# Hybrid SSD, window-attention and expert block on one core: 64-row products padded to 128 rows, and products of 64 output rows issued in turn into both halves of the array

## The chip, the cores and the metric

The kernel runs on one core of one Trainium2 chip. The metric is the device time of one execution in microseconds (us), the median of several runs. The engines are TensorE (PE; its weight loads are listed apart, as PEld), VectorE (DVE), ScalarE (ACT), GpSimd (POOL), and SyncE (SP), whose queue issues most DMAs.

## The reference, cut to what matters

One layer over 512 tokens of width 1024: an SSD branch and a window-attention branch read the same projections, their outputs are merged, and a two-of-64 mixture of experts follows. The change touches these lines of SSD (4 groups G, 8 heads J in each, head width P = 64, state N = 128, chunks of L = 128 tokens) and of attention (16 heads of width 64, 4 key/value heads, blocks of 128 tokens):

```python
    # ssd_branch
    seg = a_cum[:, :, :, None] - a_cum[:, :, None, :]
    decay = jnp.exp(jnp.where(causal, seg, -jnp.inf)).astype(xs.dtype)
    cb = jnp.einsum('bclgn,bcsgn->bclsg', cm, bm)
    y_diag = jnp.einsum('bclsgj,bcsgjp->bclgjp', cb[..., None] * decay, xdt)
    ...
    # swa_sink_branch
    scores = jnp.einsum('bnqhgd,bnkhd->bnhgqk', qb, kk).astype(jnp.float32) * ATT_SCALE
    scores = jnp.where(mask[None, :, None, None], scores, -jnp.inf)
    ...
    p = (p / denom[..., None]).astype(v.dtype)
    out = jnp.einsum('bnhgqk,bnkhd->bnqhgd', p, vv)
    ...
    # hybrid_layer
    merged = jax.nn.sigmoid(g_ssd) * y_ssd + jax.nn.sigmoid(g_att) * y_att
    x = x + merged @ w_out
    y_moe = hier_moe(h2, ...)       # 64 experts, every token goes to two
```

## The kernel before

**Stages.** The program first normalises and transposes the input (L154 to L176) and then runs the front part: projections with weights that stream in by tiles of 1 MB (`proj`, L186 to L200, and `qkv_tile`, L470 to L486), SSD by groups (`ssd_main`, L322 to L404), attention by key/value heads (`att_stage`, L557 to L632), the merge (L680 to L695) and the output projection with the router's logits (L724 to L774). Then come routing and the expert part, which streams all 64 experts' weights, 192 tiles of 1 MB, through a ring of 4 tiles `ra` and 10 tiles `rb` (L777 to L790). The `ra` and `rb` tiles lie where the front part's tiles lay, so their first loads wait until those are read for the last time.

**Products.** A projection splits operands into a high and a low part in the type fp32r and sums three products (L197 to L199, 512 columns each; L483 to L485, 256 columns each). Products in plain fp32 stand in the trace as two records for one matmul.

**Products that use part of the array.** Four places use fewer than 128 rows or fewer than 128 output rows:

- `decay` (L365), once for each of the 32 SSD heads, spreads one row of the cumulated decay over 128 partitions. The row is held as a high part in partitions 0 to 31 and a low part in 32 to 63 of `aT`, and `sel` picks and adds the two, so the product contracts over 64 rows. Its output `sb` goes through DVE (L369) and ACT (L368, L374) to a matrix `M`.
- `head` (L391): for head u (0 or 1) of pair i, four products, one for each chunk, write 64 output rows into the lower (u = 0) or upper half (u = 1) of one tile `y`. The matrix `M` is multiplied by `cbm` first, on DVE for u = 0 and on GpSimd for u = 1 (L388). One decay is made ahead (`SSD_AHEAD` = 1).
- `scores` in attention (L573, L574): a query tile holds the high part of its 64 values in one half of the partitions and the low part in the other, and L573 multiplies 128 rows of it with a doubled key tile `kT`. L574 adds the high part of the query times the low part of the key, `kL`, over 64 rows. `kL` holds the low parts of two key/value heads, one in each half.
- `weigh` (L620): for each block n, four heads (pr, u), each with the own block's weights `pc` and, for n > 0, the previous block's `pp`, write 64 output rows into half u of the tile `po[pr]`.

**Order.** The stages are written one after the other (L644 to L677), and a scheduler that works at build time mixes them: between the products of SSD and attention it puts projection products of other stages on TensorE. What order results is fixed in the program. Each engine works its own list in order.

Of the kernel before, what the change touches and what calls it, by code (L numbers as in the profile page):

```python
# [21 lines left out]
CAP, BLK, NE, NBK, STEP = 32, 128, 64, 32, 512  # L22
POOL_LO, SSD_AHEAD, NA, NB, XGT, UX = 5, 1, 4, 10, 2, 8
PAD = 800

# [6 lines left out]
def tile_hybrid(ctx: ExitStack, tc: tile.TileContext, x, pos, cols, rows, g2d, wrd, wdtd, wcm, wqkv, wso, wao, wo,  # L32
# [7 lines left out]
    def ptile(tag, bufs=2, dt=F):  # L40
        return psum.tile([128, 512], dt, name=tag, tag=tag, bufs=bufs)
# [3 lines left out]
                                      for n in ("py", "pg", "pw", "px", "pb", "pc", "pz", "pv")]  # L45
    pz.tile([128, PAD], F, name="pad")


    jp = pb.tile([128, 128], F, name="jp")
    G.iota(jp, pattern=[[1, 128]], base=0, channel_multiplier=-1, allow_small_or_imprecise_dtypes=True)  # L50
# [3 lines left out]
    V.tensor_scalar(tri, jp, 0.0, None, op0=OP.is_ge)  # L54
    trs = pb.tile([128, 128], F, name="trs")
    V.tensor_scalar(trs, jp, 0.0, None, op0=OP.is_lt)
    mcur = pb.tile([128, 128], U8, name="mcur")
    V.tensor_scalar(mcur, jp, 0.0, None, op0=OP.is_le)
    one = cp.tile([128, 1], F, name="one")
    V.memset(one, 1.0)  # L60
# [6 lines left out]
    V.memset(half, 0.5)  # L67
    sel = pb.tile([64, 32], R, name="sel")
    V.tensor_tensor(sel, ident[0:64, 0:32], ident[0:64, 32:64], op=OP.add)
    colt = pb.tile([128, 168], F, name="colt")  # L70
# [16 lines left out]
    G.iota(io4, pattern=[[STEP, 8], [1, 32]], base=0, channel_multiplier=0, allow_small_or_imprecise_dtypes=True)  # L87
    io1 = cp.tile([128, 128], F, name="io1")
    G.iota(io1, pattern=[[1, 128]], base=0, channel_multiplier=0, allow_small_or_imprecise_dtypes=True)
# [11 lines left out]
    oneb = onec.to_broadcast([128, 128])  # L101
    ltb = cp.tile([128, 128], BF, name="ltb")
    V.tensor_scalar(ltb, jp, 0.0, None, op0=OP.is_gt)
    iot = io1[:, 0:64]
    rst = cp.tile([128, 2, 17], F, name="rst")
    gts = cp.tile([128, 48], F, name="gts")
    gw = cp.tile([128, 2, 4], F, name="gw")
    ohs = cp.tile([128, 2, 256], BF, name="ohs")
# [27 lines left out]
    def y_(dt=R): return tk(py, "y", 16, 512, dt)  # L136
    def b_(dt=F): return tk(px, "b", 8, 512, dt)
    def a_(dt=F): return tk(pa, "a", 8, 512, dt)
# [68 lines left out]
    nacum = pb.tile([128, 128], F, name="nacum")  # L207
    aT = pb.tile([64, 512], R, name="aT")

# [112 lines left out]
    def ssd_main(g):  # L322
# [37 lines left out]
        def decay(i, u):  # L360
            h = 8 * g + 2 * i + u
            if u == 0:
                Es[i] = v_()
            pb_ = ptile("sb")
            T.matmul(pb_, sel[:, h:h + 1].to_broadcast([64, 128]), aT, start=True, stop=True)  # L365
            M = v_()
            us = slice(u * 64, (u + 1) * 64)
            S.activation(Es[i][us, 0:384], pb_[us, 128:512], AF.Exp)  # L368
            V.tensor_tensor(M.rearrange("p (c l) -> p c l", c=4), pb_.rearrange("p (c l) -> p c l", c=4),  # L369
                            acum.rearrange("p (c h) -> p c h", c=4)[:, :, h:h + 1].to_broadcast([128, 4, 128]),  # L370
                            op=OP.min)
            for c in range(4):
                s = slice(c * 128, (c + 1) * 128)
                S.activation(M[:, s], M[:, s], AF.Exp, bias=nacum[:, c * 32 + h:c * 32 + h + 1])  # L374
            return M

        pys = {}

        def head(i, u, M):
            ch = 4 * g + i  # L380
            if u == 0:
                pys[i] = ptile("y"), ptile("y")
                for c in range(1, 4):
                    T.matmul(pys[i][1][:, c * 128:(c + 1) * 128], prv[c][:, i * 128:(i + 1) * 128],
                             CT[:, c * 128:(c + 1) * 128], start=True, stop=True)
            py, po = pys[i]
            E = Es[i]
            (G if u else V).tensor_tensor(M, M, cbm, op=OP.mult)  # L388
            for c in range(4):
                s = slice(c * 128, (c + 1) * 128)  # L390
                T.matmul(py[u * 64:(u + 1) * 64, s], xdt[c][:, (2 * i + u) * 64:(2 * i + u + 1) * 64],  # L391
                         M[:, s], start=True, stop=True)
            if u:
                V.tensor_tensor(E[:, 0:384], po[:, 128:512], E[:, 0:384], op=OP.mult)
                y = xsT[ch]
                V.scalar_tensor_tensor(y, y, dsk[:, ch:ch + 1], py, op0=OP.mult, op1=OP.add)
                G.tensor_tensor(y[:, 128:512], y[:, 128:512], E[:, 0:384], op=OP.add)

        hs = [(i, u) for i in range(4) for u in range(2)]
        ahead = [decay(*hs[q]) for q in range(SSD_AHEAD)]  # L400
        for q in range(8):
            if q + SSD_AHEAD < 8:
                ahead.append(decay(*hs[q + SSD_AHEAD]))
            head(*hs[q], ahead.pop(0))  # L404

# [112 lines left out]
    def kv_stage():  # L518
# [3 lines left out]
        for kv in range(4):  # L522
            p = ptile("tp")
            for t in range(4):
                src = kn[t // 2][:, (t % 2) * 256 + kv * 64:(t % 2) * 256 + kv * 64 + 64]
                T.transpose(p[0:64, t * 128:(t + 1) * 128], src, ident)

            k_ = b_(R)
            for u in range(2):
                S.activation(k_[u * 64:u * 64 + 64], p[0:64], AF.Copy)  # L530
            kT.append(k_)
            if kv % 2 == 0:
                kL.append(b_(R))
            V.tensor_tensor(kL[-1][kv % 2 * 64:kv % 2 * 64 + 64], p[0:64], k_[0:64].bitcast(F), op=OP.subtract)

# [21 lines left out]
    def att_stage(kv):  # L557
# [3 lines left out]
        def scores(n):  # L561
# [5 lines left out]
            ks = slice(max(n - 1, 0) * 128, max(n - 1, 0) * 128 + 256)  # L567
            hs = slice(kv % 2 * 64, kv % 2 * 64 + 64)
            for u in range(2):
                sc = ptile("sb")  # L570
                for pr in range(2):
                    o, q_ = sc[:, pr * 256:pr * 256 + 256], qT[2 * pr + u]
                    T.matmul(o, q_[:, ns], kT[kv][:, ks], start=True, stop=False)  # L573
                    T.matmul(o, q_[hs, ns], kL[kv // 2][hs, ks], start=False, stop=True)  # L574
                s3 = sc.rearrange("p (r k) -> p r k", r=2)
# [15 lines left out]
        def weigh(n, pm, sm):  # L591
# [21 lines left out]
            for pr in range(2):  # L613
                for u in range(2):
                    o = po[pr][u * 64:(u + 1) * 64, ns]
                    hs = slice((2 * pr + u) * 128, (2 * pr + u + 1) * 128)
                    for w, (pk, nn) in enumerate(((pc, n), (pp, n - 1))):
                        if pk is None:
                            continue
                        T.matmul(o, vt[nn // 2][:, (nn % 2) * 256 + kv * 64:(nn % 2) * 256 + kv * 64 + 64],  # L620
                                 pk[:, hs], start=(w == 0), stop=(w == 1 or n == 0))

# [668 lines left out]
```

## Time and profile before

| | us |
|---|---|
| median of 3 runs | 1267.71 (1267.61 to 1268.23) |
| the profiled execution, its own time | 1267.16 |
| its span in the trace | 1265.4 |
| TensorE busy, by the page | 1177.4 (93%) |
| DVE / ACT / GpSimd busy, by the page | 651.2 / 388.6 / 237.8 |

The columns of a timeline are the start in us from the span's start, the time taken in us, the engine, the line, the operation, what it writes and reads, its shape, and the number of records that are merged into the row. Matmuls follow each other in a pipeline: a record's own duration is longer than the distance to the next record's start. What a matmul costs is therefore read as the distance from its start to the next start.

### The profile page before, as it was taken

Reading aid. Unit: us, or ns where it says so; the run is one execution under the profiler, and the core shown is the slowest. Engines: PE = TensorE matmul, PEld = TensorE weight load, DVE = VectorE, ACT = ScalarE, POOL = GpSimd, SP = SyncE. Lnnn points to the kernel's source line nnn. Section 1 sums busy time; section 2 is a strip of 40 time slices with the busy share of each in tenths; the row PEclk is TensorE's granted clock in tenths of the full one; section 3 lists DMA queues with packets and bytes.
Section 4 is the critical chain, followed back from the end, with each engine's and each line's share of the span. In section 5 each row is a group of like instructions: output and inputs, shape, how many; then the busy total and the mean of one; then the engine's idle time right before and its main releaser. Section 6 shows DMA issues by size and latency. Waiting matters only on the chain.

```text
span 1265.4 us, 16578 instructions
## 1 busy us (share of the span) xinstructions
PE 1177.4 (93%) x6552; PEld 789.3 (62%) x6552; DVE 651.2 (51%) x1224; ACT 388.6 (31%) x796; POOL 237.8 (19%) x189
## 2 busy tenths in 40 slices
PE   6999999999999999999999996989899799989885
PEld 5877878877888878887777994442424244424321
DVE  5956565568526667766647446443342234232422
ACT  5455453454326444534423330210111011101100
POOL 2033431143024522240020131010001000000000
PEclk9999999999999999999999997999999999999998
DMA  4321213211220222212145717999999999999995
GB/s 167 105 89 38 97 67 117 100 67 57 76 101 34 100 68 84 76 64 78 43 167 188 294 55 296 420 415 420 420 419 419 419 416 388 385 414 418 419 419 235
DMA packets 43120, 273.86 MB, mean 216 GB/s; under 512 B 5024, under 2 KB 5664, under 8 KB 11808
## 3 DMA queue, kind: packets, MB, share of 16 engines
q1 hardware_dynamic: 39744, 263.34, 52.7%
q0 software_dynamic: 1712, 7.34, 1.5%
q10 hardware_dynamic: 1584, 2.10, 0.6%
q8 instruction: 52, 0.85, 0.3%
q14 instruction: 28, 0.23, 0.1%
HBM read 266.47 MB, written 6.29 MB: 216 GB/s over the span
## 4 chain that ended last, share of the span: by engine, by line
PE 52%; DMA 6%; DVE 5%; ACT 1%; issue 1%; DVEq 0%; SPq 0%
PE mm L908 10%; PE y L929 6%; PE tp L888 5%; PE mm L197 4%; PE mm L198 4%; PE mm L199 4%; DMA rb<-in_wdn_dram 4%; PE tp L1007 3%; DVE acc L1009 2%; PE tp L1008 2%; PE sb L574 2%; DMA ra<-in_wdn_dram 2%; PE y L620 1%; PE sb L573 1%; PE mm L483 1%; PE mm L485 1%
## 5 line engine op out<-in xcount | busy, mean ns | idle before, releaser
L197 PE MATMUL mm<-h,g 128*128 128x512 f32 x448 | 180.7, 403 | 1.3 <-DVE c L309 1.0
L199 PE MATMUL mm<-h,g 128*128 128x512 f32 x448 | 178.3, 398 | 0.8 <-POOL g L183 0.7
L198 PE MATMUL mm<-h,g 128*128 128x512 f32 x448 | 178.2, 398 | 0.0
L908 PE MATMUL mm<-rb,st 128*32 128x512 f32 x712 | 144.7, 625 | 9.8 <-DMA rb<-in_wgu_dram 9.8
L182 ACT ACTIVATE g<-w 128x1024 fp32r<-128x1024 f32 x100 | 105.6, 1057 | 157.0 <-PE mm L198 113.1
L183 DVE TENSOR_TENSOR g<-w,g 128x1024 fp32r<-128x1024 f32 x78 | 96.8, 1240 | 70.4 <-ACT g L182 66.4
L1009 DVE TENSOR_TENSOR acc<-acc,tp 128x512 f32<-128x512 f32 x132 | 85.9, 684 | 34.4 <-PE tp L1008 34.3
L997 POOL TENSOR_SCALAR wk<-dr,vcol 128x512 fp32r<-128x512 int16 x17 | 26.6, 1565 | 385.4 <-PE tp L1008 347.9
L197 PEld LDWEIGHTS mm<-h,g 128*128 128x128 f32 x448 | 84.4, 188 | 22.7 <-issue 3.8
L199 PEld LDWEIGHTS mm<-h,g 128*128 128x128 f32 x448 | 84.2, 188 | 21.5 <-issue 2.3
L198 PEld LDWEIGHTS mm<-h,g 128*128 128x128 f32 x448 | 84.4, 188 | 18.8 <-issue 2.8
L183 POOL TENSOR_TENSOR g<-w,g 128x1024 fp32r<-128x1024 f32 x22 | 53.8, 2447 | 174.9 <-ACT g L182 143.6
L929 PE MATMUL y<-rb,n 128*32 128x512 f32 x384 | 77.0, 673 | 5.2 <-ACT n L920 3.3
L908 PEld LDWEIGHTS mm<-rb,st 128*32 128x32 f32 x712 | 31.3, 114 | 73.6 <-issue 55.0
L888 PEld LDWEIGHTS tp<-oh,hx 128*128 128x128 f32 x480 | 61.3, 194 | 22.3 <-issue 14.9
L935 DVE TENSOR_TENSOR yo<-y,yo 128x512 fp32r<-128x512 f32 x34 | 23.5, 691 | 99.0 <-ACT yo L934 99.0
L908 PE MATMUL mm<-ra,st 128*32 128x512 f32 x312 | 73.1, 596 | 0.0
L1007 PE MATMUL tp<-yo,wk 128*128 128x512 f32 x132 | 59.2, 465 | 12.7 <-DVE acc L1009 12.5
L888 PE MATMUL tp<-oh,hx 128*128 128x256 f32 x480 | 67.4, 293 | 3.6 <-DVE m L960 3.6
L1007 PEld LDWEIGHTS tp<-yo,wk 128*128 128x128 f32 x132 | 23.6, 187 | 68.9 <-DVE acc L1009 39.5
L913 ACT ACTIVATE n<-mm,rst 128x256 f32<-128x256 f32 x17 | 8.0, 473 | 177.0 <-PE mm L908 169.4
L484 PE MATMUL mm<-g,h 128*128 128x256 f32 x192 | 55.1, 287 | 0.9 <-DVE g L183 0.8
(375 smaller groups left out, 2257.5 us busy)
## 6 DMA issues: line engine op xcount, KB each, us to landing
rb<-in_wgu_dram SPq DMA_DIRECT2D x89, 1024.0 KB, 14.0
rb<-in_wdn_dram SPq DMA_DIRECT2D x48, 1024.0 KB, 16.9
ra<-in_wgu_dram SPq DMA_DIRECT2D x39, 1024.0 KB, 12.2
w<-in_wcm_dram SPq DMA_DIRECT2D x27, 1024.0 KB, 4.9
ra<-in_wdn_dram SPq DMA_DIRECT2D x16, 1024.0 KB, 16.6
w<-in_wso_dram SPq DMA_DIRECT2D x8, 1024.0 KB, 4.9
w<-in_wqkv_dram SPq DMA_DIRECT2D x6, 1024.0 KB, 4.9
gtd<-c POOLq DMA_DIRECT2D x16, 256.0 KB, 2.5
```

Source lines behind the costliest of these rows:

```text
L182: S.activation(hi[:, :n], src, AF.Copy)
L183: (G if nsp[0] < 3 or nsp[0] % POOL_LO == 0 else V).tensor_tensor(lo[:, :n], src, hi[:, :n].bitcast(F), op=OP.subtract)
L197: T.matmul(p, hi[:, s], mh[k], start=(k == 0), stop=False)
L198: T.matmul(p, hi[:, s], ml[k], start=False, stop=False)
L199: T.matmul(p, lo[:, s], mh[k], start=False, stop=(k == 7))
L484: T.matmul(o, hh[k][:, ts], lo[:, s], start=False, stop=False)
L888: T.matmul(p[:, u * 256:(u + 1) * 256], hx[h][:, t, (k + u) * 128:(k + u + 1) * 128], oh[:, t], start=(h == 0 and t == 0), stop=(h == 1 an ...
L908: T.matmul(pg[e * 32:(e + 1) * 32], sts[u // 2][:, k, c:c + 32], wt[u, k // 4, e][:, (k % 4) * 512:(k % 4 + 1) * 512], start=(k == 0), sto ...
L929: T.matmul(py[n][e * 32:(e + 1) * 32], hT[:, f * 128 + e * 32:f * 128 + e * 32 + 32], wt[u, 2, e][:, ws], start=(f == 0), stop=(f == 1))
L997: G.tensor_scalar(wk, drow[0], vcol[:, b:b + 1], None, op0=OP.is_equal)
L1007: T.matmul(p, wk[:, t * 128:(t + 1) * 128], yhl[n][0], start=True, stop=False)
L1009: V.tensor_tensor(acc[t][:, ns], acc[t][:, ns], p, op=OP.add)
```

## The change

- `sel` and `aT` get 128 rows; the upper 64 are filled with zeros by GpSimd. The decay product (L365) contracts over 128 rows.
- Each key/value head gets its own `kL` of 128 rows, whose other half is filled with zeros by GpSimd (four new memsets of 64x512). L574 becomes a product over all 128 rows (L571 of the changed file).
- `head` becomes `heads`: both `M` of a pair are multiplied first, and then the eight products of the pair are issued in turn, lower half, upper half, chunk by chunk. Two decays of the next pair are written ahead instead of one.
- `weigh` loops over u inside, so that its products also alternate between the halves.
- For room and by the way: the tile `pad` goes, the pool of `b` tiles grows from 8 to 10, `trs` becomes bf16, `jp` and `io1` share a tile, `rst` lies in `gts`, and `ltb` is made earlier.

The diff, cut:

```diff
-    sel = pb.tile([64, 32], R, name="sel")
-    V.tensor_tensor(sel, ident[0:64, 0:32], ident[0:64, 32:64], op=OP.add)
+    sel = pb.tile([128, 32], R, name="sel")
+    G.memset(sel.bitcast(F), 0.0)
+    V.tensor_tensor(sel[0:64], ident[0:64, 0:32], ident[0:64, 32:64], op=OP.add)
...
-    io1 = cp.tile([128, 128], F, name="io1")
+    io1 = jp
     G.iota(io1, pattern=[[1, 128]], base=0, channel_multiplier=0, allow_small_or_imprecise_dtypes=True)
...
-    aT = pb.tile([64, 512], R, name="aT")
+    aT = pb.tile([128, 512], R, name="aT")
+    G.memset(aT[64:128].bitcast(F), 0.0)
...
-            T.matmul(pb_, sel[:, h:h + 1].to_broadcast([64, 128]), aT, start=True, stop=True)
+            T.matmul(pb_, sel[:, h:h + 1].to_broadcast([128, 128]), aT, start=True, stop=True)
...
-        def head(i, u, M):
+        def heads(i, Ms):
...
-            (G if u else V).tensor_tensor(M, M, cbm, op=OP.mult)
+            for u in range(2):
+                (G if u else V).tensor_tensor(Ms[u], Ms[u], cbm, op=OP.mult)
             for c in range(4):
                 s = slice(c * 128, (c + 1) * 128)
-                T.matmul(py[u * 64:(u + 1) * 64, s], xdt[c][:, (2 * i + u) * 64:(2 * i + u + 1) * 64],
-                         M[:, s], start=True, stop=True)
...
+                for u in range(2):
+                    T.matmul(py[u * 64:(u + 1) * 64, s], xdt[c][:, (2 * i + u) * 64:(2 * i + u + 1) * 64],
+                             Ms[u][:, s], start=True, stop=True)
...
+        both = lambda i: [decay(i, u) for u in range(2)]
+        nxt = both(0)
+        for i in range(4):
+            cur, nxt = nxt, both(i + 1) if i < 3 else None
+            heads(i, cur)
...
-            if kv % 2 == 0:
-                kL.append(b_(R))
-            V.tensor_tensor(kL[-1][kv % 2 * 64:kv % 2 * 64 + 64], p[0:64], k_[0:64].bitcast(F), op=OP.subtract)
+            kl, h = b_(R), kv % 2 * 64
+            G.memset(kl[64 - h:128 - h].bitcast(F), 0.0)
+            V.tensor_tensor(kl[h:h + 64], p[0:64], k_[0:64].bitcast(F), op=OP.subtract)
+            kL.append(kl)
...
-                    T.matmul(o, q_[hs, ns], kL[kv // 2][hs, ks], start=False, stop=True)
+                    T.matmul(o, q_[:, ns], kL[kv][:, ks], start=False, stop=True)
...
-                for u in range(2):
-                    o = po[pr][u * 64:(u + 1) * 64, ns]
-                    hs = slice((2 * pr + u) * 128, (2 * pr + u + 1) * 128)
-                    for w, (pk, nn) in enumerate(((pc, n), (pp, n - 1))):
-                        if pk is None:
-                            continue
-                        T.matmul(o, vt[nn // 2][:, (nn % 2) * 256 + kv * 64:(nn % 2) * 256 + kv * 64 + 64],
-                                 pk[:, hs], start=(w == 0), stop=(w == 1 or n == 0))
+                for w, (pk, nn) in enumerate(((pc, n), (pp, n - 1))):
+                    if pk is None:
+                        continue
+                    for u in range(2):
+                        T.matmul(po[pr][u * 64:(u + 1) * 64, ns],
+                                 vt[nn // 2][:, (nn % 2) * 256 + kv * 64:(nn % 2) * 256 + kv * 64 + 64],
+                                 pk[:, (2 * pr + u) * 128:(2 * pr + u + 1) * 128], start=(w == 0), stop=(w == 1 or n == 0))
```

How the instructions stand on TensorE, before, at the third pair of heads of SSD's first group. Output tile `y`, then the matrix (`v`) and the chunk's tokens (`x`) that are read; `v_753` is the matrix of the lower half, `v_770` that of the upper half, and `mm` is a projection's product:

```order
L391 MATMUL y_777<-v_753,x_635 64x128
L391 MATMUL y_777<-v_753,x_636 64x128
L391 MATMUL y_777<-v_753,x_637 64x128
L391 MATMUL y_777<-v_753,x_638 64x128
L197 MATMUL mm_1093<-h_212,g_1089 128x512
L391 MATMUL y_777<-v_770,x_635 64x128
L391 MATMUL y_777<-v_770,x_636 64x128
L391 MATMUL y_777<-v_770,x_637 64x128
L391 MATMUL y_777<-v_770,x_638 64x128
```

The same pair after the change, where `v_742` belongs to the lower half and `v_751` to the upper half:

```order
L390 MATMUL y_795<-v_742,x_634 64x128
L196 MATMUL mm_1092<-h_210,g_1088 128x512
...
L196 MATMUL mm_1092<-h_228,g_1088 128x512
L390 MATMUL y_795<-v_751,x_634 64x128
L390 MATMUL y_795<-v_742,x_635 64x128
L390 MATMUL y_795<-v_751,x_635 64x128
L390 MATMUL y_795<-v_742,x_636 64x128
L390 MATMUL y_795<-v_751,x_636 64x128
L390 MATMUL y_795<-v_742,x_637 64x128
L390 MATMUL y_795<-v_751,x_637 64x128
```

The first product of the pair now stands apart from the rest, with seven projection products between, and the other seven follow in turn. Of the 16 pairs, ten stand in one piece after the change; six are cut: three like this one, two into pieces of one, five and two products, and one into one, one and six. Before, nine of the 16 stood in one piece, lower half first, three as two pieces of four, three as pieces of three and five, and one as three, one and four. The runs of such products number 24 before and 25 after for SSD, and 18 before and 16 after for attention.

On GpSimd, before, while the keys and the first queries are normalised (`c` are tiles of that normalisation, L126 its power, L498 its factor, L183 a projection's low part):

```order
L126 TENSOR_TENSOR c<-c,mh_100 128x8
L498 TENSOR_TENSOR c<-c,rowt 128x512
L183 TENSOR_TENSOR g<-w,g 128x1024
L126 TENSOR_TENSOR c<-c,mh_100 128x8
L498 TENSOR_TENSOR c<-c,rowt 128x512
```

And after the change, at the same place:

```order
L125 TENSOR_TENSOR c<-c,mh_101 128x8
L530 MEMSET b 64x512 x2
L495 TENSOR_TENSOR c<-c,rowt 128x512
L182 TENSOR_TENSOR g<-w,g 128x1024
L125 TENSOR_TENSOR c<-c,mh_101 128x8
L530 MEMSET b 64x512 x2
L495 TENSOR_TENSOR c<-c,rowt 128x512
```

Two pairs of the new memsets of `kL` stand between a power and its factor. On TensorE 256 of 5437 instructions stand in another place than before, most of them by a few products. SyncE's list of loads keeps its order but for one tile of the expert part, which moves by four places.

## Rows read from the trace of the kernel before

**Rows 1.** The page: engines over the span; TensorE's granted clock in 40 slices, in tenths.

```profile
PE 1177.4 (93%) x6552; PEld 789.3 (62%) x6552; DVE 651.2 (51%) x1224; ACT 388.6 (31%) x796; POOL 237.8 (19%) x189
...
PEclk9999999999999999999999997999999999999998
```

**Rows 2.** Busy time by stretch: PE, PEld, DVE, ACT, POOL, PEclk, DMA share, GB/s.

```profile
0.00:760.00 760.00, 743.69 (x4057) 602.22 (x4058) 468.58 (x844) 333.17 (x692) 205.04 (x166) 1.00 0.28 98
...
510.00:553.00 43.00, 43.00 (x315) 36.48 (x313) 31.23 (x76) 20.87 (x60) 14.72 (x9) 1.00 0.16 57
...
800.00:1245.00 445.00, 395.39 (x2244) 164.50 (x2243) 152.33 (x285) 51.12 (x95) 29.93 (x21) 0.96 1.00 414
```

**Rows 3.** The longest of TensorE's waits, 0 to 760: us in total, times, longest.

```profile
PE tp L170 <- DVE x L164: 9.3, 3, 8.1
```

**Rows 4.** One group on TensorE, 0 to 760: count | busy us, mean ns | idle before.

```profile
L574 PE MATMUL sb<-b,x 64*128 64x256 f32 x64 | 24.4, 381 | 0.0
```

**Rows 5.** TensorE in order of time around attention's scores: start us, us, instruction.

```profile
512.92 0.28 PE L485 MATMUL mm<-g,h 128*128 128x256 f32 x1
...
513.96 0.28 PE L485 MATMUL mm<-g,h 128*128 128x256 f32 x1
...
640.17 0.28 PE L573 MATMUL sb<-b,x 128*128 128x256 f32 x1
...
642.57 0.50 PE L197 MATMUL mm<-h,g 128*128 128x512 f32 x1
642.91 0.39 PE L198 MATMUL mm<-h,g 128*128 128x512 f32 x1
```

**Rows 6.** TensorE in order of time around projections and one decay broadcast.

```profile
98.00 0.39 PE L199 MATMUL mm<-h,g 128*128 128x512 f32 x1
...
98.46 0.40 PE L198 MATMUL mm<-h,g 128*128 128x512 f32 x1
...
100.16 0.40 PE L197 MATMUL mm<-h,g 128*128 128x512 f32 x1
100.48 0.49 PE L365 MATMUL sb<-aT,sel 64*128 64x512 f32 x1
...
101.24 0.40 PE L199 MATMUL mm<-h,g 128*128 128x512 f32 x1
```

**Rows 7.** TensorE in order of time around writes to one half or both.

```profile
105.70 1.58 PE L391 MATMUL y<-v,x 128*64 128x128 f32 x16
107.22 0.50 PE L365 MATMUL sb<-aT,sel 64*128 64x512 f32 x1
...
113.07 1.09 PE L391 MATMUL y<-v,x 128*64 128x128 f32 x8
114.09 0.50 PE L197 MATMUL mm<-h,g 128*128 128x512 f32 x1
114.52 1.09 PE L391 MATMUL y<-v,x 128*64 128x128 f32 x8
...
478.11 0.66 PE L620 MATMUL y<-v,b 128*64 128x128 f32 x8
478.69 0.38 PE L573 MATMUL sb<-b,x 128*128 128x256 f32 x1
...
607.16 1.36 PE L620 MATMUL y<-v,b 128*64 128x128 f32 x16
608.45 0.66 PE L604 MATMUL tp<-ident,v 128*128 128x128 f32 x4
```

**Rows 8.** GpSimd: one product of SSD in time, and a group.

```profile
107.47 1.29 POOL L388 TENSOR_TENSOR v<-v 128x512 f32<-128x512 f32 x1 [5.71 <-ACT v L374]
...
L565 POOL MEMSET v<- 128x512 f32 x4 | 2.1, 530 | 9.3 <-DVE v L601 9.3
```

**Rows 9.** SyncE's queue in order of time at the start of the expert weights.

```profile
714.70 41.12 SPq L783 DMA_DIRECT2D rb<-in_wgu_dram  x4
755.97 1.90 SPq L783 DMA_DIRECT2D rb<-in_wdn_dram  x4
```

More of the change, by code (lines that the diff above doesn't have):

```diff
@@ L22 @@
 CAP, BLK, NE, NBK, STEP = 32, 128, 64, 32, 512
-POOL_LO, SSD_AHEAD, NA, NB, XGT, UX = 5, 1, 4, 10, 2, 8
-PAD = 800
+POOL_LO, NA, NB, XGT, UX = 5, 4, 10, 2, 8
 def _rows(ap, n, parts=128):
@@ L45, in tile_hybrid @@
                                       for n in ("py", "pg", "pw", "px", "pb", "pc", "pz", "pv")]
-    pz.tile([128, PAD], F, name="pad")
-    jp = pb.tile([128, 128], F, name="jp")
+    jp = cp.tile([128, 128], F, name="jp")
     G.iota(jp, pattern=[[1, 128]], base=0, channel_multiplier=-1, allow_small_or_imprecise_dtypes=True)
@@ L54, in tile_hybrid @@
     V.tensor_scalar(tri, jp, 0.0, None, op0=OP.is_ge)
-    trs = pb.tile([128, 128], F, name="trs")
+    trs = pb.tile([128, 128], BF, name="trs")
     V.tensor_scalar(trs, jp, 0.0, None, op0=OP.is_lt)
@@ L58, in tile_hybrid @@
     V.tensor_scalar(mcur, jp, 0.0, None, op0=OP.is_le)
+    ltb = cp.tile([128, 128], BF, name="ltb")
+    V.tensor_scalar(ltb, jp, 0.0, None, op0=OP.is_gt)
     one = cp.tile([128, 1], F, name="one")
@@ L101, in tile_hybrid @@
     oneb = onec.to_broadcast([128, 128])
-    ltb = cp.tile([128, 128], BF, name="ltb")
-    V.tensor_scalar(ltb, jp, 0.0, None, op0=OP.is_gt)
     iot = io1[:, 0:64]
-    rst = cp.tile([128, 2, 17], F, name="rst")
     gts = cp.tile([128, 48], F, name="gts")
+    rst = gts[:, 0:34].rearrange("p (c q) -> p c q", c=2)
     gw = cp.tile([128, 2, 4], F, name="gw")
@@ L136, in y_, with b_ @@
     def y_(dt=R): return tk(py, "y", 16, 512, dt)
-    def b_(dt=F): return tk(px, "b", 8, 512, dt)
+    def b_(dt=F): return tk(px, "b", 10, 512, dt)
     def a_(dt=F): return tk(pa, "a", 8, 512, dt)
@@ L375, in decay @@
             return M
-        pys = {}
-        def head(i, u, M):
+        def heads(i, Ms):
             ch = 4 * g + i
[L381 to L386, printed above, removed]
+            py, po = ptile("y"), ptile("y")
+            for c in range(1, 4):
+                T.matmul(po[:, c * 128:(c + 1) * 128], prv[c][:, i * 128:(i + 1) * 128],
+                         CT[:, c * 128:(c + 1) * 128], start=True, stop=True)
@@ L387, in head @@
             E = Es[i]
-            (G if u else V).tensor_tensor(M, M, cbm, op=OP.mult)
+            for u in range(2):
+                (G if u else V).tensor_tensor(Ms[u], Ms[u], cbm, op=OP.mult)
             for c in range(4):
                 s = slice(c * 128, (c + 1) * 128)
-                T.matmul(py[u * 64:(u + 1) * 64, s], xdt[c][:, (2 * i + u) * 64:(2 * i + u + 1) * 64],
-                         M[:, s], start=True, stop=True)
[L393 to L404, printed above, removed]
+                for u in range(2):
+                    T.matmul(py[u * 64:(u + 1) * 64, s], xdt[c][:, (2 * i + u) * 64:(2 * i + u + 1) * 64],
+                             Ms[u][:, s], start=True, stop=True)
+            V.tensor_tensor(E[:, 0:384], po[:, 128:512], E[:, 0:384], op=OP.mult)
@@ L406, in ssd_norm @@
+            y = xsT[ch]
+            V.scalar_tensor_tensor(y, y, dsk[:, ch:ch + 1], py, op0=OP.mult, op1=OP.add)
+            G.tensor_tensor(y[:, 128:512], y[:, 128:512], E[:, 0:384], op=OP.add)
+        both = lambda i: [decay(i, u) for u in range(2)]
[3 more added lines that the diff above has]
+            heads(i, cur)
     def ssd_norm(g):
@@ L567, in scores @@
             ks = slice(max(n - 1, 0) * 128, max(n - 1, 0) * 128 + 256)
-            hs = slice(kv % 2 * 64, kv % 2 * 64 + 64)
             for u in range(2):
```

## The prediction

> **What bounds the kernel now.** I read the page first, then the busy time by stretch, TensorE's waits, TensorE in order of time, and last SyncE's queue. The page shows TensorE at 93% of the span and its clock at 9 in nearly every slice, so time on TensorE is priced at its higher level, 2.4 GHz [rows 1]. The stretches split the run in two. Up to 760 us TensorE is busy 743.69 of 760, DVE 468.58; from 800 us on the DMA share is 1.00 at 414 GB/s [rows 2]. The front part is thus TensorE's and the expert part the weight stream's. Of the 16.3 us that TensorE idles in front, 9.3 are the first transposes' wait [rows 3]; the scores' 64-row products have no idle before them [rows 4]. But "busy" here hides something: it counts a matmul's own duration, and in the distance from start to start the products with 64 rows or 64 output rows cost far more than their columns. The expert stream cannot start sooner than the front part ends: SyncE sits 41.12 us in the loads of `rb`, until 755.97 [rows 9], and its list of waits names the output projection's products as the cause. Whatever the front part loses therefore comes off the end, as far as no other engine steps in.
>
> **Scores (L573, L574).** Nine products of 256 columns in the full array take 513.96 - 512.92 = 1.04 us, 0.116 each [rows 5]. The eight products of one block of attention, where full and 64-row products alternate, take 642.57 - 640.17 = 2.40 us, and the projection product behind them another 0.34 [rows 5], where two projection products otherwise take 98.46 - 98.00 = 0.46, 0.23 each [rows 6]. Padded to 128 rows they are eight ordinary products, 8 x 0.116 = 0.93 us. So a group of four pairs saves 2.40 + 0.11 - 0.93 = 1.58 us, 0.39 a pair, of which each change of the row count costs about 0.2. There are 64 pairs [rows 4], in 26 runs by the order. A run's first full product has no change ahead of it, but its last 64-row product has the 0.11 behind it; the two cancel. 64 x 0.39 = **25.0 us**. The padding itself costs nothing on TensorE, as time goes by columns there, not by rows.
>
> **Decay (L365).** From the projection product ahead of a decay to the second one behind it 101.24 - 100.16 = 1.08 us pass for three products of 512 columns, against 3 x 0.23 = 0.69 [rows 6]. The 32 decays stand in 28 places (four are doubled). 28 x 0.39 = **10.9 us**.
>
> **SSD's heads (L391).** Eight records in one half take 114.09 - 113.07 = 1.02 us; sixteen, eight in the lower half and then eight in the upper, 107.22 - 105.70 = 1.52, so the halves overlap a little already; eight records that alternate, matmul by matmul, 478.69 - 478.11 = 0.58 [rows 7]. Between 0.58 for four steps and 1.02 for eight lies 0.11 a step, and a pair of records in both halves costs one step: a run of n steps takes 0.14 + 0.11 n. Before: nine pairs at 1.52, three at 2 x 1.02, three at 0.80 + 1.02, one at 0.80 + 0.36 + 1.02, together 27.4 us (pieces of three products are six steps, of one two). After: ten pairs in one piece of eight steps at 1.02, three at 0.36 + 1.02, one at 0.36 + 0.36 + 0.80, two at 0.36 + 0.80 + 0.36, together 18.9. One run more costs 0.2 for entering and leaving. **8.3 us** saved.
>
> **Attention's weighted sums (L620).** Four of the 16 blocks alternate already (0.58). Of the other twelve, nine take 608.45 - 607.16 = 1.29 [rows 7], one already alternates by twos, for which I put 1.07, and two stand in pieces at 0.58 + 1.02 and 0.2 for the second run. After, all twelve stand in one piece of eight steps at 1.02: 9 x 0.27 + 0.05 + 2 x 0.78 = **4.1 us**.
>
> The four terms make 25.0 + 10.9 + 8.3 + 4.1 = 48.3 us.
>
> The Trainium skill (TensorE: Matmul & The Clock Gate, Part 3) says that a weight load overlaps matmuls in flight only when it goes to another group of rows. The two halves here share all rows; by that rule alternating would bring nothing, and the sum would be 35.9. The row of 0.58 for eight records that alternate, against 1.02 in one half, speaks against it.
>
> **What may eat of it.** Operands have to keep up with a faster TensorE. One product of GpSimd for an upper half ends at 107.47 + 1.29 = 108.76 [rows 8], and its records start at 114.52 [rows 7]: 5.8 us of cover, where such a stretch gets some 2 us shorter. In attention's second stage, 510 to 553, DVE works 31.23 of 43 us [rows 2], while TensorE's share shrinks by 16 x 0.39 and about 2 us to some 35, still above DVE. In `heads` the upper half's first product now stands ahead of most of the lower half's, so TensorE, with the projections queued behind it, waits for GpSimd's product if that is late; the order answers by putting projection products between. The four memsets of `kL` cost at most 4 x 0.53 = 2.1 us [rows 8], of which the order puts two pairs between a power and its factor, where DVE works in between anyway; I take 0.5. The memsets of `sel` and `aT` and the iota into `jp` lie at the start, where GpSimd is done long before its first power. The bf16 `trs`, the tiles' new places and SyncE's one moved load I put at nothing: they hang on DVE's slack and on a ring that keeps its order; a moved load may cost or gain about one load, 2.5 us at 414 GB/s. For uncovered operands I bound the loss by one GpSimd product, 1.29 us, in each of the eight stages of SSD and attention: 0 to 10.3 us. I take 1.8, nearer to nothing, as the cover of 5.8 us is the nearer row. Together 2.3 us are lost and 46.0 stay.
>
> **Sum.** 1267.16 of the profiled execution minus 46.0 is 1221.2. The median of the runs lies 0.55 above that execution: **1221.7 us**.
>
> **Rivals.**
> - *Other engines become the bound.* The list is fixed, so an operand that comes late stops all behind it. For it speaks DVE's load in the attention stages; against it the cover above. With the whole 10.3 us lost and the memsets uncovered the gain is 48.3 - 12.4 = 35.9 and the time 1231.8.
> - *The halves don't overlap in SSD and in the sums*, the rule above: 12.4 us less gained, 1234.1 with the same losses. The two matrices of a pair are different tiles, while the alternating rows of 0.58 read one tile; but 1.52 for sixteen records of two matrices is already below 2 x 1.02.
> - *The change doesn't bring its gain to the end.* If the expert stream were bound by something that does not move with the front part, nothing is won: 1267.7. SyncE's wait until 755.97 speaks against it.
> - *Slower.* Each of the 16 pairs now needs both matrices before its second product. If GpSimd's product came after TensorE got there, every pair would wait; from 48.3 / 16 = 3.0 us a pair all gain is gone. For that GpSimd would have to be 5.8 + 3.0 us later than now; at 4 us a pair the time is 1267.7 + 16 = 1284.
>
> **How the numbers follow.** The forecast 0.76; others as the bound 0.15; no overlap 0.03; nothing at the end 0.03; slower 0.02; the rest, 0.01, a gain past 51 us. The range reaches down by the bounds of my rows (0.39 a pair is good to about 0.03, 2 us over 64; no loss at all, 2.3 us) and the moved load, to 1216, and up to 1234, past the case of other engines and up to that of no overlap. Faster by over 0.2% (2.5 us, about what a measurement of this kernel can tell from no change) 0.95, within it 0.03, slower 0.02.
>
> **What would show it.** In the changed kernel's trace the score products should follow each other at 0.12 us, a decay at 0.23, and both halves should take 1.02 for sixteen records in one run. The `rb` loads should end their wait near 710 us instead of 756. The DVE chain of the routing, and the stream from there to the end, should last as long as now. Idle time on TensorE behind DVE or GpSimd in attention would mean the first rival; a front part shorter by 46 us with a later end, the third. The prediction is wrong if padding to 128 rows leaves a cost that the ordinary products don't have.

## The result, and the profile after

| | before | after |
|---|---|---|
| median of 4 runs each, same chip, us | 1267.66 | 1229.97 (1228.64 to 1230.21) |
| ratio, 95% interval | | 0.9705 [0.9693, 0.9717] |
| profiled execution / its span, us | 1267.16 / 1265.4 | 1228.64 / 1226.8 |

The change gains 37.7 us; the forecast was 46.0 and 1221.7 us. Of the forecast gain 8.3 us are missing; the question is where they are.

Engines over the span, and TensorE's granted clock in 40 slices, of the changed kernel (it answers [rows 1]): TensorE is 41.1 us less busy, DVE 5.3 more.

```profile
PE 1136.3 (93%) x6552; PEld 772.2 (63%) x6552; DVE 656.5 (54%) x1224; ACT 388.6 (32%) x796; POOL 239.3 (20%) x195
...
PEclk9999999999999999999999989999999899999999
```

Busy time by stretch of the changed kernel, columns as in [rows 2]: front part and expert part. The front part is still TensorE's, and the stream moves 416 GB/s, where it moved 414.

```profile
0.00:720.00 720.00, 703.30 (x4040) 584.05 (x4041) 471.44 (x835) 331.14 (x686) 203.39 (x168) 1.00 0.29 101
760.00:1205.00 445.00, 394.81 (x2265) 166.07 (x2264) 152.51 (x285) 51.85 (x96) 29.92 (x21) 0.97 1.01 416
```

SyncE's queue of the changed kernel at the start of the expert weights (it answers [rows 9]). The second row's start is the best mark in the trace for the length of the front part: it stood at 755.97 and stands at 719.85, so the front part is 36.1 us shorter. What follows takes 1226.8 - 719.85 = 507.0 us; it took 509.4.

```profile
678.58 41.12 SPq L779 DMA_DIRECT2D rb<-in_wgu_dram  x4
719.85 1.87 SPq L779 DMA_DIRECT2D rb<-in_wdn_dram  x4
```

TensorE in order of time in the changed kernel, at three places (start us, us, instruction, records merged). First a group of four score pairs with the projection behind it ([rows 5] before): eight products in 599.20 - 598.24 = 0.96 us, where they took 2.40. Then a decay between projections ([rows 6]): 99.85 - 99.62 = 0.23, no more than a projection product. Then the sixteen records of a pair of heads ([rows 7]): 105.42 - 104.40 = 1.02, and the twelve runs of sixteen records of the weighted sums take 1.02 too. All three are what the prediction wrote.

```profile
598.24 0.28 PE L570 MATMUL sb<-b,x 128*128 128x256 f32 x1
598.36 0.29 PE L571 MATMUL sb<-b,x 128*128 128x256 f32 x1
...
599.08 0.28 PE L571 MATMUL sb<-b,x 128*128 128x256 f32 x1
599.20 0.39 PE L196 MATMUL mm<-h,g 128*128 128x512 f32 x1
...
99.62 0.40 PE L365 MATMUL sb<-aT,sel 128*128 128x512 f32 x1
99.85 0.39 PE L198 MATMUL mm<-h,g 128*128 128x512 f32 x1
...
104.40 1.09 PE L390 MATMUL y<-v,x 128*64 128x128 f32 x16
105.42 0.49 PE L365 MATMUL sb<-aT,sel 128*128 128x512 f32 x1
```

**Waiting did not take the gain.** TensorE's waits in the front part of the changed kernel, longest first (engine, line, for whom: us, times, longest). Beside the old 9.6 us of the first transposes [rows 3] two are new, 1.5 us for the diagonal of `ssd_norm` and 0.4 us of the scores; all that the view lists sum to 16.5 us, before to 14.8. The scores' 0.4 is the only wait in attention's scores and sums, and `heads` has none.

```profile
PE tp L169 <- DVE x L163: 9.6, 3, 8.3
PE sb L414 <- DVE v L412: 1.5, 1, 1.5
...
PE sb L570 <- DVE v L576: 0.4, 1, 0.4
```

**What did get slower is work that the change does not touch.** TensorE in order of time in the changed kernel, nine projection products in a row, in a place without anything between them. Eight distances are 205.54 - 203.67 = 1.87 us, 0.234 each. Before, two such products took 0.46 [rows 6], 0.230 each.

```profile
203.67 0.39 PE L196 MATMUL mm<-h,g 128*128 128x512 f32 x1
...
205.54 0.39 PE L198 MATMUL mm<-h,g 128*128 128x512 f32 x1
```

Over all places where such products of `h` or `x` follow each other, the mean distance is 229.6 ns before (some 1380 of them) and 234.1 after (some 1400). The 256-column products of attention's projections, which take `h` as weights, go from 115.9 to 119.9. With 28 tiles of 48 products in the first projections and 4 in attention's output (1536) and 6 tiles of 96 in queries, keys and values (576) that is 1536 x 4.5 + 576 x 4.0 ns = 9.2 us: about what is missing. The products that read `y` tiles take 227 ns (median) in both kernels. A periodic pattern in the distances (226, 229, 232 ns over and over before; seven values from 230 to 238 after) spoke against other engines' work as the cause.

### The profile page after: what moved, and what is told of

It is laid out like the page before. It is cut to its first block, busy times and chain, and to the rows that moved or that the text cites. A ratio compares the mean times of both kernels' runs of the same rounds, so it can differ in the third digit from the quotient of the medians.

```text
span 1226.8 us, 16583 instructions
## 1 busy us (share of the span) xinstructions
PE 1136.3 (93%) x6552; PEld 772.2 (63%) x6552; DVE 656.5 (54%) x1224; ACT 388.6 (32%) x796; POOL 239.3 (20%) x195
## 4 chain that ended last, share of the span: by engine, by line
PE 77%; DVE 10%; DMA 8%; issue 2%; ACT 2%; POOL 1%; SPq 0%; DVEq 0%; ACTq 0%; POOLq 0%
PE mm L196 11%; PE mm L198 11%; PE mm L197 11%; PE mm L904 11%; PE y L925 5%; PE tp L884 5%; DMA rb<-in_wgu_dram 3%; PE tp L1003 3%; DVE acc L1005 2%; PE mm L481 2%; PE tp L1004 2%; PE mm L480 2%; DMA ra<-in_wdn_dram 2%; DMA rb<-in_wdn_dram 2%; PE mm L482 2%
## 5 line engine op out<-in xcount | busy, mean ns | idle before, releaser
L925 PE MATMUL y<-rb,n 128*32 128x512 f32 x384 | 72.0, 641 | 4.0 <-ACT n L916 3.3
L909 ACT ACTIVATE n<-mm,gts 128x256 f32<-128x256 f32 x17 | 8.0, 473 | 180.6 <-PE mm L904 161.7
L910 DVE SCALAR_TENSOR_TENSOR n<-n,mm 128x256 f32<-128x256 f32 x17 | 7.1, 421 | 92.6 <-ACT n L909 92.6
```

The source lines that it names most:

```text
L925: T.matmul(py[n][e * 32:(e + 1) * 32], hT[:, f * 128 + e * 32:f * 128 + e * 32 + 32], wt[u, 2, e][:, ws], start=(f == 0), stop=(f == 1))
```

## The experiments

### Where the tiles lie

The change moved tiles: `jp` and `ltb` went into the first pool, `io1` and `rst` lost their own place. So the tiles `x`, `h` and `a` behind them lie 160 bytes lower in each partition. By the addresses of the built programs, given here as the remainder by 256: the weights `g` and the tiles `y` are at 224 in both kernels, `h` and `x` at 32 before and at 128 after. Five kernels move only this, by one unused tile:

```diff
-    ixx = cp.tile([128, 3], I32, name="ixx")
+    ixx = cp.tile([128, 3], I32, name="ixx"); cp.tile([128, 8], F, name="shift")
```

(8, 16 and 24 floats in e1, e2 and e3; 24 and 48 in e4 and e5, where the pad tile is smaller by 32 and 64). Each engine's order is the same.

> The changed kernel with the h, x and a tiles moved by 32 bytes in each partition (an unused tile ahead of them); the instructions and their order are the same. In the kernel before these tiles start 32 bytes past a multiple of 128, in the changed one at a multiple of 128. Theory P (place): the missing 8 us are the projection products, which follow each other at 234 ns in the changed kernel and at 229 before, and the place of the tiles that they read sets this. Then 512-column products go back to 229-230 ns and the 256-column ones that take h as weights from 120 to 116: about 1536 x 4.5 ns + 576 x 4 ns = 9.2 us less, some 1221 us. Rival O (other work): the products are slower because the changed order puts more work of DVE, GpSimd or DMA beside them. Then nothing moves: 1230 within 1 us, 234 ns.

> As the run with 32 bytes, moved by 64 bytes: a place that no kernel so far had. Theory P: a pace of its own, somewhere from 227 to 234 ns, so 1219 to 1230 us; it says only that the pace is one number for all h and x tiles and differs from run to run of this series. Rival O: 1230 within 1 us, 234 ns.

> As the run with 32 bytes, moved by 96 bytes, so that h and x lie 96 bytes past a multiple of 128 as the y tiles do in both kernels, whose products follow each other at 227 ns. Theory P: 512-column products of h and x at 227-228 ns, 256-column ones with h as weights stay at 120: 1536 x 7 ns = 10.8 us less, some 1219 us. Rival O: 1230 within 1 us.

> The kernel before with h, x and a moved by 96 bytes to a multiple of 128, as in the changed kernel, and the pad tile 128 bytes smaller; instructions and order as before. Theory P: the kernel before loses what the changed one lost: 512-column products at 234 ns, 256-column ones with h as weights at 120, about 9.2 us more, some 1277 us, and against this kernel the change gives the 46 to 48 us that the instructions alone were priced at. Rival O: 1267.7 within 1 us.

> The kernel before with h, x and a moved by 192 bytes to 224 past a multiple of 256, where the weights lie and where the fastest run of the changed kernel (1221.1 us) has them; pad tile 256 bytes smaller, order as before. Theory P+T (the instructions and the place add): against that fastest run the kernel before loses what it loses at the other place, 44.6 us, so 1265 to 1267 us; by the paces, 1536 products of 512 columns 1 to 2 ns faster and 576 of 256 columns 3.7 ns slower than in the kernel before, it stands within 1.5 us of that kernel. Rival: the place matters only beside the changed instructions; then the kernel before gains or loses nothing at any place, which the run with the tiles at 0 speaks against already.

Measured (the fifth column is the start of the first `rb` load of a `wdn` tile on SyncE, the mark used above; the last two are means over the starts of such products):

| kernel | h, x at | median us | ratio to before | front part ends | 512 columns, ns | 256 columns, ns |
|---|---|---|---|---|---|---|
| before | 32 | 1267.66 | | 755.97 | 229.6 | 115.9 |
| e4, before | 128 | 1274.57 | 1.0055 [1.0038, 1.0072] | 764.34 | 234.1 | 119.8 |
| e5, before | 224 | 1265.67 | 0.9982 [0.9966, 0.9998] | 757.32 | 228.4 | 119.6 |
| after | 128 | 1229.97 | 0.9705 [0.9693, 0.9717] | 719.85 | 234.1 | 119.9 |
| e1, after | 160 | 1226.53 | 0.9678 [0.9662, 0.9694] | 717.64 | 233.3 | 117.2 |
| e2, after | 192 | 1225.80 | 0.9671 [0.9655, 0.9688] | 717.12 | 233.1 | 117.1 |
| e3, after | 224 | 1221.06 | 0.9628 [0.9612, 0.9644] | 712.60 | 228.4 | 119.6 |

The place decides. The kernel before, with its tiles where the changed kernel has them, loses 764.34 - 755.97 = 8.4 us of front part, and 6.9 us of the whole time; theory P said about 9.2, and the rival had it unmoved. The change itself is then worth 764.34 - 719.85 = 44.5 us, and at 224 it is 757.32 - 712.60 = 44.7; the whole times give 44.6 at both places. SyncE's queue in e4 and e5, and then in e3:

```profile
764.34 1.87 SPq L783 DMA_DIRECT2D rb<-in_wdn_dram  x4
...
757.32 1.87 SPq L783 DMA_DIRECT2D rb<-in_wdn_dram  x4
```

```profile
712.60 1.84 SPq L779 DMA_DIRECT2D rb<-in_wdn_dram  x4
```

TensorE in order of time in e3, the same stretch as above: 205.62 - 203.81 = 1.81 us for eight distances, 0.226 each, where the changed kernel has 0.234.

```profile
203.81 0.39 PE L197 MATMUL mm<-h,g 128*128 128x512 f32 x1
...
205.62 0.39 PE L196 MATMUL mm<-h,g 128*128 128x512 f32 x1
```

One expectation failed outright: e1 was to go back to 229 ns and 1221 us and came to 233.3 ns and 1226.5. It took the remainder by 128 for what counts; 160 and 32 agree in that, and their paces don't. e3 (1221.06 for some 1219) and e4 (1274.57 for some 1277) moved the way that was expected, by some 2 us less. e3 beats both kernels, and its interval does not touch the changed kernel's.

### The price of one array shape after another, and the map of places

A kernel without the layer, for TensorE alone: `full` and `part` are a product over 128 and over 64 rows, `m` and `s` move the start of the moving tile and of the weights.

```python
...
for m in range(0, 64, 8):             # in floats: 0 to 224 bytes
    for s in range(0, 64, 8):
        for n in range(24):
            full(n, m, s)
        sep()                         # two small products
for word in ("F", "L", "FL", "FLLF", "FFLL", "FFFFL"):   # 40 products of 256 columns each
    ...
for word in ("0", "01", "00001111", "0011"):             # 32 fp32 products of 64 output rows
    ...
```

> A measurement of TensorE alone: the layer is left out, the products run over zeros and the output is not the layer's. First 64 chains of 24 fp32r products of 512 columns, in which the moving tile and the weights each start 0 to 224 bytes past a multiple of 256, in steps of 32; then chains of 256-column products over 128 rows (F) and 64 rows (L) in the patterns F, L, FL, FLLF, FFLL, FFFFL; 512-column ones in F and FFL; and fp32 products of 64 output rows in the lower half alone, in turn (01), by twos and by fours. Theory P (place): with every other engine idle the 512-column products still differ by place; with weights at 224: moving at 224 gives 227 ns, at 128 234, at 160 and 192 233, at 32 229 or 233. If the place of one against the other decides, the diagonal of the map is 227 throughout; if each counts by itself, a row or a column stands out. Rival O (other work): all chains take the same. Theory T (a change of the row count costs 0.2 us, not the product itself): F and L alone 0.116 us each, FL (0.39 + 0.23) / 2 = 0.31, FLLF and FFLL about 0.21, FFFFL 0.19, FFL of 512 columns 0.36. Rival L: the 64-row product itself costs 0.5 us: L 0.5, and FLLF as much as FL. Halves: one half alone 0.13 us a record, in turn 0.07, 0011 and 00001111 between.

Other engines do nothing here, and the paces still differ, so rival O is out. They depend on the distance alone: the eight chains that share the remainder (weights - moving) by 256 agree within 0.7 ns (1.4 ns at 128), wherever both lie (one execution). Means of the last 15 distances of each chain, over eight chains:

| weights - moving, mod 256 | 0 | 32 | 64 | 96 | 128 | 160 | 192 | 224 |
|---|---|---|---|---|---|---|---|---|
| ns a product | 227.0 | 233.3 | 233.4 | 234.2 | 232.5 | 233.3 | 228.9 | 233.3 |

Busy time over the map (columns as in [rows 2]: only TensorE works), and two of its chains with the separator behind each. With weights at 224, 24 products take 252.48 - 246.78 = 5.70 us with the moving tile at 128 (distance 96), and 391.54 - 385.96 = 5.58 us with it at 224 (distance 0):

```profile
20.00:391.00 371.00, 371.00 (x1667) 303.02 (x1666) 0.00 (x0) 0.00 (x0) 0.00 (x0) 1.00 0.00 1
...
246.78 5.87 PE L54 MATMUL p<-mv,st 128*128 128x512 f32 x24
252.48 0.30 PE L51 MATMUL q<-mv,st 128*128 128x64 f32 x2
...
385.96 5.74 PE L54 MATMUL p<-mv,st 128*128 128x512 f32 x24
391.54 0.30 PE L51 MATMUL q<-mv,st 128*128 128x64 f32 x2
```

The kernels fit: distance 192 before (228.9 here, 229.6 there), 96 after (234.2 and 234.1), 64 in e1, 32 in e2 (233.3, 233.4 and 233.3, 233.1), 0 in e3 and for `y` (227.0 here; 228.4 and a median of 227 there). The means in the kernels count the first products of a chain too, and at distance 0 those take 224 to 236 ns before the chain settles at 226 to 227, here and in e3.

The 256-column chains, TensorE in order of time (start us, us, instruction, records; place 0 for both operands). F: 40 products in 4.87 us to the separator, 0.122 each; L, over 64 rows: 4.99, 0.125. So a 64-row product by itself costs what a full one costs. FL: 402.63 - 402.32 = 0.31 each, so every change of the row count adds 0.19.

```profile
391.68 5.04 PE L54 MATMUL p<-mv,st 128*128 128x256 f32 x40
396.55 0.31 PE L51 MATMUL q<-mv,st 128*128 128x64 f32 x2
396.79 5.06 PE L58 MATMUL p<-mv,st 64*128 64x256 f32 x40
401.78 0.41 PE L51 MATMUL q<-mv,st 128*128 128x64 f32 x2
402.02 0.36 PE L54 MATMUL p<-mv,st 128*128 128x256 f32 x1
402.32 0.38 PE L58 MATMUL p<-mv,st 64*128 64x256 f32 x1
402.63 0.38 PE L54 MATMUL p<-mv,st 128*128 128x256 f32 x1
...
406.08 0.58 PE L58 MATMUL p<-mv,st 64*128 64x256 f32 x1
406.58 0.58 PE L54 MATMUL p<-mv,st 128*128 128x256 f32 x1
```

From 406 us on the granted clock is lower, so FLLF and FFLL can't be set beside these numbers; a run below does that in the real kernel. The chains into halves run at the full clock again. One half alone: (494.50 - 487.37) / 64 = 0.111 us a record; in turn (01): 3.64 / 64 = 0.057; by fours 4.47 / 64 = 0.070; by twos 3.69 / 64 = 0.058. The expectation had one half at 0.13 and in turn at 0.07, both too high, and twos between the two; by twos is as good as in turn.

```profile
487.37 7.20 PE L86 MATMUL p<-ff 128*64 128x128 f32 x64
494.50 0.41 PE L51 MATMUL q<-mv,st 128*128 128x64 f32 x2
494.84 3.71 PE L86 MATMUL p<-ff 128*64 128x128 f32 x64
498.48 0.41 PE L51 MATMUL q<-mv,st 128*128 128x64 f32 x2
498.82 4.54 PE L86 MATMUL p<-ff 128*64 128x128 f32 x64
503.29 0.41 PE L51 MATMUL q<-mv,st 128*128 128x64 f32 x2
503.63 3.77 PE L86 MATMUL p<-ff 128*64 128x128 f32 x64
507.32 0.41 PE L51 MATMUL q<-mv,st 128*128 128x64 f32 x2
```

### One part undone at a time

Four kernels undo one part of the change each; tiles, their places and the padding stay. TensorE's order stays in u1 and u2; in u3 and u4 the scheduler mixes anew.

```diff
-                    T.matmul(o, q_[:, ns], kL[kv][:, ks], start=False, stop=True)       # u1; h: the 64 rows of the head
+                    T.matmul(o, q_[h, ns], kL[kv][h, ks], start=False, stop=True)
...
-            T.matmul(pb_, sel[:, h:h + 1].to_broadcast([128, 128]), aT, ...)            # u2
+            T.matmul(pb_, sel[0:64, h:h + 1].to_broadcast([64, 128]), aT[0:64], ...)
...
-            for c in range(4):                                                          # u3
-                for u in range(2):
+            for u in range(2):
+                for c in range(4):
...
-                for w, (pk, nn) in enumerate(((pc, n), (pp, n - 1))):                   # u4
-                    for u in range(2):
+                for u in range(2):
+                    for w, (pk, nn) in enumerate(((pc, n), (pp, n - 1))):
```

> The changed kernel with the scores' second product over 64 rows again (tiles, padding and order of the instructions as in the changed kernel). Theory T (the prediction's term): 64 pairs x 0.39 us = 25.0 us more, some 1255 us. Rival W: part of what the scores gained is given back as waiting of TensorE for other engines in attention; then undoing it costs less, 12 to 20 us, 1242 to 1250.

> The changed kernel with the decay's product over 64 rows again (sel and aT keep 128 rows, order unchanged). Theory T: 28 places x 0.39 us = 10.9 us more; here the two decays of a pair stand closer together, so that some share their changes of the row count: 28 down to 16 places, 6 to 11 us, some 1239 us. Rival W: the decays run ahead of work that waits for DVE and ACT anyway, 0 to 4 us more, under 1234.

> The changed kernel with the loops over heads and chunks exchanged in SSD: four products of the lower half, then four of the upper one (the scheduler mixes the order around them anew). Theory T: the halves run beside each other only where they alternate; 8 us more, some 1238 us. Rival N: sixteen records in a row take nearly the same either way, under 3 us more, under 1233.

> The changed kernel with attention's weighted sums by halves again (both products of one half, then both of the other). Theory T: 4 us more, some 1234 us. Rival N: under 1.5 us.

| undone | median us | ratio to before | front part ends | costs, us | forecast term |
|---|---|---|---|---|---|
| nothing (after) | 1229.97 | 0.9705 [0.9693, 0.9717] | 719.85 | | |
| u1, scores | 1253.20 | 0.9891 [0.9866, 0.9916] | 744.90 | 25.05 | 25.0 |
| u2, decay | 1238.89 | 0.9778 [0.9753, 0.9803] | 728.44 | 8.6 | 10.9 |
| u3, heads | 1236.39 | 0.9760 [0.9733, 0.9787] | 726.60 | 6.8 | 8.3 |
| u4, sums | 1234.13 | 0.9737 [0.9713, 0.9761] | 725.77 | 5.9 | 4.1 |

The costs are differences of the front part's end, one profile each. The whole times say the same less sharply (23.2, 8.9, 6.4 and 4.2), because what follows takes between 505.1 and 510.7 us in the twelve profiles, up and down without regard to the edits. Rivals W and N fall in all four. The expectation of u2 had a wrong count: the 32 decays stand in 26 places of its order, not in 16. SyncE's queue in u1, u2, u3 and u4, in this order:

```profile
744.90 1.92 SPq L779 DMA_DIRECT2D rb<-in_wdn_dram  x4
...
728.44 1.84 SPq L779 DMA_DIRECT2D rb<-in_wdn_dram  x4
...
726.60 1.90 SPq L779 DMA_DIRECT2D rb<-in_wdn_dram  x4
...
725.77 1.87 SPq L779 DMA_DIRECT2D rb<-in_wdn_dram  x4
```

In u2 one can count what TensorE pays. Along its list up to the output projection there are 274 neighbours of different array shape before, 92 after, 220 in u1, 137 in u2. That is 25.05 / 128 = 0.196 us a change in u1 and 8.6 / 45 = 0.19 in u2. For the decays of the kernel before, 274 - 92 - 128 = 54 changes, it makes some 10.3 us, an estimate, against a term of 10.9.

The last run, u5, keeps the 64-row products of u1 and groups them: of each two pairs the second goes 64 rows first, then the full rows. The scheduler also mixes the order around them anew.

```diff
-                    T.matmul(o, q_[:, ns], kT[kv][:, ks], start=True, stop=False)
-                    T.matmul(o, q_[h, ns], kL[kv][h, ks], start=False, stop=True)
+                    for full in ((True, False), (False, True))[pr]:
+                        T.matmul(o, q_[:, ns] if full else q_[h, ns], kT[kv][:, ks] if full else kL[kv][h, ks],
+                                 start=full == (pr == 0), stop=full == (pr == 1))
```

> The changed kernel with the scores' second product over 64 rows again, but with the second pair of each two issued the other way round (full, 64, 64, full rows): as many 64-row products as in the run with scores over 64 rows (1253.2 us), in 34 stretches of 64-row products instead of 64. Theory T (each change of the row count costs, 0.39 us for in and out): 30 x 0.39 = 11.7 us less than that run, some 1241.5 us. Rival L (each 64-row product costs): as that run, 1253 within 1.5 us.

It took 1241.91 us (0.9795 [0.9775, 0.9815]), 11.3 less than u1, where 11.7 were expected. Its list has 60 changes of shape fewer than u1's, which makes 11.4 us at 0.19 each. By the end of the front part (the row below) it gains more, 744.90 - 731.04 = 13.9; with the order around the scores changed too, the 2.6 us between the two readings are not assigned.

```profile
731.04 1.87 SPq L779 DMA_DIRECT2D rb<-in_wdn_dram  x4
```

Of one group in time, TensorE in u5 and then in u1: the same eight products take 606.20 - 604.48 = 1.72 us with four changes of shape, and 622.62 - 620.23 = 2.39 with eight.

```profile
604.48 1.88 PE L571 MATMUL sb<-b,x 128*128 128x256 f32 x8
606.20 0.40 PE L196 MATMUL mm<-h,g 128*128 128x512 f32 x1
```

```profile
620.23 0.28 PE L570 MATMUL sb<-b,x 128*128 128x256 f32 x1
620.43 0.38 PE L571 MATMUL sb<-b,x 64*128 64x256 f32 x1
...
622.31 0.38 PE L571 MATMUL sb<-b,x 64*128 64x256 f32 x1
622.62 0.50 PE L196 MATMUL mm<-h,g 128*128 128x512 f32 x1
```

(The first row merges records of both shapes under the shape of its first.) Rival L, a price for each 64-row product, falls.

## Why the prediction was right, and where 8 us went

- **What bounds the kernel**: right. What TensorE saves in the front part comes off the end; after the mark the run takes as long as before, within the scatter. The mark itself was forecast near 710 and stands at 719.85, in e3 at 712.60.
- **Scores**: right, 25.05 for 25.0, and for the reason given: a change of the row count costs 0.2 us, not the product. The Trainium skill (TensorEngine Tiling (Array Packing), Key Properties) says that changing the tiling mode drains TensorE; the rows agree in that each change costs time, and give it a price, 0.19 us.
- **Decay**: right in kind, some 10.3 by the price of a change (u2, with other neighbours, measured 8.6). The term took all 28 places at two full changes of 0.195; the counts leave 54 for 56, at 0.19.
- **Heads and sums**: 6.8 and 5.9 for 8.3 and 4.1, together 12.7 for 12.4. The undone orders are not the old ones, since the scheduler mixes anew, so the split between the two is rough. The rival that the halves don't overlap is out: alternation takes 0.057 us a record, one half alone 0.111. What the prediction drew for it from a rule of the Trainium skill (TensorE: Matmul & The Clock Gate, Part 3), that alternating brings nothing when both halves share all rows, is not what these rows show.
- **What eats of it**: 2.3 us forecast. The four parts sum to 25.05 + 10.3 + 6.8 + 5.9, some 48.0, and 44.5 arrive at an unchanged place: 3.5 us, of which the list of waits shows 1.7. By the whole times the parts sum to 23.2 + 10.3 + 6.4 + 4.2 = 44.1, for 44.6 of the change, so whether anything beyond the waits is lost stays open. The memsets of `kL` were not measured apart.
- **The tiles' new places**: here the prediction failed. They stand in its list of things put "at nothing: they hang on DVE's slack and on a ring that keeps its order". It asked only whether a tile would be free in time. Where it starts costs 8.4 us of front part, since some 2100 products that the change never touched each take about 4 ns more. Of the 46.0 forecast 44.5 came at an unchanged place, and 44.5 - 8.4 = 36.1 is the front part's gain as measured; the rest of the 37.7 lies behind it, in the part that scatters.
- **The first rival** (other engines become the bound, 1231.8) came nearest in time, and is wrong as a cause: TensorE waits 1.7 us more than before.
- **The range**: that 1229.97 lies in 1216 to 1234 is luck in part. Its upper end was set by two rivals that did not come, and the loss that came is none of those that it allowed for. Its lower end is not the sum of the bounds given for it: 2 + 2.3 + 2.5 = 6.8 us below 1221.7 is 1214.9.

Open: why the distance between weights and moving tile matters was not tried. Neither was why, in the kernel before, the first three chains of `proj`, from 28 to 45 us, run at 233 ns at a place where the products ahead of them and all later ones run at 229; the place alone does not explain those.

## What to carry to other kernels

Price a small matmul by the changes of array shape around it (0.19 us each here): pad it to the full shape, or put products of one shape side by side, and issue halves in turn (by twos did as well, 0.058 against 0.057). When an edit adds or drops a tile, compare the start addresses of what TensorE reads: the pace of untouched products can move by 3%, and for 512 columns it was best here with weights and moving tile at the same remainder by 256 bytes. To find such a thing, compare the distance between starts of the same products in both traces before looking for waits.

## What the runs showed that was not expected

- fp32r products of 512 columns take 227 to 234 ns by the place of weights against moving tile, with all other engines idle; those of 256 columns 116 to 120, with another distance as the best of the five places tried in the layer (weights 32, moving 224: 115.9).
- In a chain that alternates row counts TensorE's clock fell although the engine was never idle. Busy time by stretch in the kernel for TensorE alone (columns as in [rows 2]): in both stretches TensorE is busy throughout, but from 406 us on, while FL goes on, the granted clock is 0.50, the lower level of 1.2 GHz; at 487 us, behind 512-column products, it is 1.00 again. This is one fall in one execution, and that the alternation caused it was not tried apart; in the layer, where such products stand in short groups, the clock stayed at 1.00 to 760 us [rows 2]. At the lower level a change of the row count costs more, 0.30 us (FL 0.51 a product, two F in a row 0.21).

```profile
402.00:406.00 4.00, 4.00 (x15) 2.40 (x14) 0.00 (x0) 0.00 (x0) 0.00 (x0) 1.00 0.00 0
407.00:435.00 28.00, 28.00 (x70) 17.82 (x69) 0.00 (x0) 0.00 (x0) 0.00 (x0) 0.50 0.00 1
```
